# Two dense expert loops: the order of their VectorE and ScalarE work around the gate multiply

## The chip, the cores and the metric

The kernel runs on one core of a Trainium2 chip. The metric is the device time of a launch in microseconds: 2806.3 us, the median of three runs (2805.26 to 2808.78). The engines are named TensorE (PE; PEld is its weight load), VectorE (DVE), ScalarE (ACT), GpSimd (POOL) and SyncE (SP). Each engine works through its own instructions in order and waits at the head of its queue.

## The reference, cut to what matters

Two layers, each a token mixer and then PEER, a feed-forward part with 16384 experts. A token picks 128 experts (8 heads, 16 each):

```python
eidx = jnp.take_along_axis(cidx, pos, axis=-1)
gate = jax.nn.softmax(best, axis=-1)
ue = jnp.take(u, eidx, axis=0)
ve = jnp.take(v, eidx, axis=0)
act = jax.nn.gelu(jnp.einsum('td,thkd->thk', xc, ue).astype(jnp.float32)) * gate
return jnp.einsum('thk,thkd->td', act.astype(xc.dtype), ve)
```

u and v are 16384 x 1024 in float32. Layer 0 has 512 tokens (256 of the context, 256 latent), layer 1 only the 256 latent ones.

## The kernel before

The kernel does most tokens **densely**: the gates are spread into a matrix over all experts that is zero where an expert wasn't picked, and then all 16384 experts are computed for all tokens, 128 experts at a time. `dense` does this in 128 steps n. In layer 0 three tiles of 128 tokens go this way (nd = 3, 384 columns) and the fourth is gathered; in layer 1 both tiles are dense (nd = 2, 256 columns).

The matmuls take float32 in pieces: a value x becomes a high part, which ScalarE writes as a rounded copy, and a low part, which VectorE writes as x less the high part. `mm3` (L109 to L111) adds three products: high by high, high by low, low by high. One step n has these parts:

- `part(n)`: uh (ScalarE, L719) and ul (VectorE, L720) from 128 x 1024 values of u; two buffers each.
- `dots(n)`: 24 matmuls of u with the tokens' high and low parts into the tile mm.
- `act(n)`: ScalarE writes c = gelu(mm) (L735).
- `gated(n)`: VectorE multiplies c by the gates (L903); then ch (ScalarE, L65) and cl (VectorE, L73); two buffers each.
- `partv(n)`: vh (ScalarE, L880) and vl (VectorE, L881) from v. vh has three buffers; vl has two in layer 0 and three in layer 1.
- `second(n)`: 18 matmuls in layer 0 and 12 in layer 1, of ch and cl with vh and vl, added up in PSUM over all 128 steps. The first load of each three takes ch, the second matmul vl, the third load cl.

The order within a loop is written out by hand (`manual_schedule`). Step n issues dots(n+3) and act(n+3), gated(n+1), part(n+5), second(n) and partv(n+2).

**Stashed columns.** For some n, c was computed before the loop, in gaps of earlier stages, and kept in DRAM: 20 in layer 0 (n = 10, 11, 22, 23, 36, 37, 48, 49, 62, 63, 74, 75, 86, 87, 100, 101, 112, 113, 126, 127) and 32 in layer 1 (6, 7, 14, 15 and so on to 126, 127). They come in pairs; for them the loop leaves part and dots out and SyncE loads c (L873).

**Gather steps.** In layer 0 the fourth tile's experts are gathered, one row pair of u and v a token, in 131 gather steps put between the dense steps. A gather step e takes a piece of the top-k work for the next head (`pick`), adds v of an earlier expert (`accum`, VectorE, L827), starts a gather (`fetch`, GpSimd, L811) and takes the dot product of the tokens with a gathered row of u (`dot`, VectorE, L817), whose sum two small ScalarE instructions turn into a coefficient (L818, L819). After each dense step a formula says how many of them are issued: one after most, none after some, two after the steps 6, 31, 46, 70, 95 and 110. The last item is `combine` for this tile, with its transposes on TensorE, after step 124.

SyncE loads u and v two steps at a time, 1024 KB each (L711, L862), into a ring of five buffers that both share, and the gates (L868).

Of the kernel before, what the change touches and what calls it, by code (L numbers as in the profile page):

```python
# [37 lines left out]
class Kern:  # L38
# [664 lines left out]
    def first_half(self, l, ND, hh, hl, b):  # L703
# [10 lines left out]

        def part(n, eng=None):

            t, x = U.pop(n)
            uh, ul = b([128, 8, 128], F32R, tag="uh", bufs=2), b([128, 8, 128], F32R, tag="ul", bufs=2)
            nc.scalar.activation(uh, t[:, x], AF.Copy)  # L719
            (eng or nc.vector).tensor_tensor(ul, t[:, x], uh.bitcast(F32), op=ALU.subtract)  # L720
            return uh, ul

# [14 lines left out]

        return load, part, dots, act, hold

    def dense(self, l, t0, nd, hh, hl, IX, GA, first, stash, waits, spare, ng, gather):  # L740
# [3 lines left out]
        with ExitStack() as st:  # L744
# [43 lines left out]

            gsteps = []
            if gather:  # L790
# [23 lines left out]
                def dot(e):  # L814
                    x = UV[e]
                    a = gp([128, 1], F32, tag="act", bufs=3)
                    nc.vector.scalar_tensor_tensor(x[:, 0:1024], x[:, 0:1024], 1.0, htok, op0=ALU.mult, op1=ALU.mult, accum_out=a)  # L817
                    nc.scalar.activation(a, a, AF.Gelu_apprx_tanh)  # L818
                    nc.scalar.activation(a, a, AF.Copy, scale=gGA[:, e:e + 1])  # L819
                    ACT[e] = a  # L820

                def accum(e):
                    x, a = UV.pop(e)[:, 1024:2048], ACT.pop(e)
                    if e == 0:
# [51 lines left out]

            def partv(n):
                vh, vl = b2([128, 1024], F32R, tag="vh", bufs=3), b2([128, 1024], F32R, tag="vl", bufs=2 if nd == 3 else 3)
                v = V.pop(n)
                nc.scalar.activation(vh, v, AF.Copy)  # L880
                nc.vector.tensor_tensor(vl, v, vh.bitcast(F32), op=ALU.subtract)  # L881
                return vh, vl

# [6 lines left out]
            with self.tc.manual_schedule():  # L890
# [8 lines left out]

                def gated(n):  # L900
                    c = C.pop(n)
                    cv = c.rearrange("p (c t) -> p c t", t=32)
                    nc.vector.tensor_mul(cv, cv, GT.pop(n))  # L903
                    ch, cl = b2([128, ND], F32R, tag="ch", bufs=2), b2([128, ND], F32R, tag="cl", bufs=2)
                    self.split(c, ch, cl)
                    S[n] = (ch, cl)

                for n in range(3):
                    C[n] = act(dots(P.pop(n)))
                    P[n + 2] = part(n + 2)  # L910
                    if n < 2:
                        VV[n] = partv(n)
                for n in range(128):
                    loadg(n + 4)
                    loadv(n + 4)
                    if n + 6 not in late:
                        load(n + 6)
                    if n == 0:
                        gated(0)
                    if n + 3 < 128 and n + 3 not in late:  # L920
                        C[n + 3] = act(dots(P.pop(n + 3)))
                    if n + 1 < 128:
                        gated(n + 1)
                    if n + 5 < 128 and n + 5 not in late:
                        P[n + 5] = part(n + 5)
                    second(n, S.pop(n), VV.pop(n))
                    if n + 2 < 128:
                        VV[n + 2] = partv(n + 2)
                    spent += 0.9 if n in late else 2
                    while gsteps and ns - len(gsteps) < (ns + 2) * spent / total:  # L930
                        gsteps.pop(0)()
            for x in gsteps:
                x()
# [298 lines left out]
```

## Time and profile before

| | |
|---|---|
| median of 3 runs | 2806.3 us |
| the profiled execution | 2807.95 us, of which its span is 2806.2 us |
| TensorE busy | 2673.5 us (95%) |
| its weight loads | 2305.6 us (82%) |
| VectorE | 2028.2 us (72%) |
| ScalarE | 1412.6 us (50%) |
| GpSimd | 572.8 us (20%) |
| granted TensorE clock | 0.985 of full speed |

Busy shares are means over stages with different limits: the two dense loops are the stretches from 718 to 1708 us and from 2181 to 2796 us, and each has to be read for itself. A matmul's end is modelled and overlaps the next one's start, so how TensorE paces is best read from the starts of its weight loads. In brackets behind a row stands the time in which the engine was idle before that instruction, and what ended it.

### The profile page before, as it was taken

To read this page: it belongs to the slowest core of one execution; us is meant where nothing else is said; L and a number is where in the kernel's file an instruction comes from. 1 tells how busy PE (TensorE), PEld (TensorE's weight loads), DVE (VectorE), ACT (ScalarE), POOL (GpSimd) and SP (SyncE) were. 2 spreads that over 40 slices of the span, in tenths; PEclk is the share of its full clock that TensorE was granted. 3 is DMA by queue.
4 is the path that set the end of the run, shared out by engine and by line. 5 is a ranking of instruction groups with operands and counts; after the bars stand their busy time and mean duration, and the time that the engine had idled before them with its cause. 6 is when DMAs were issued, how large, how long until landed. Compare 5 with 4: busy or idle time off the path is not lost.

```text
span 2806.2 us, 40422 instructions
## 1 busy us (share of the span) xinstructions
PE 2673.5 (95%) x15043; PEld 2305.6 (82%) x15043; DVE 2028.2 (72%) x4323; ACT 1412.6 (50%) x2528; POOL 572.8 (20%) x538
## 2 busy tenths in 40 slices
PE   7999999999999999999999998998889999999998
PEld 4677778798988888898898896657789888888887
DVE  4688559999677787787878776656987655555555
ACT  5756543399444344444344436444388444444444
POOL 0000023288122222221222221005366000000000
PEclk9999999999999999999999999999999999999999
DMA  6334223445788878887778782354346665666653
GB/s 257 126 135 149 91 79 147 150 195 225 271 296 300 302 272 300 299 303 280 283 289 313 298 298 77 120 216 148 124 184 253 240 220 212 226 233 220 218 216 126
DMA packets 155204, 609.68 MB, mean 217 GB/s; under 512 B 10752, under 2 KB 90368, under 8 KB 90880
## 3 DMA queue, kind: packets, MB, share of 16 engines
q1 hardware_dynamic: 136576, 472.87, 46.0%
q0 software_dynamic: 18432, 134.23, 13.1%
q8 instruction: 119, 1.95, 0.3%
q14 instruction: 77, 0.63, 0.1%
HBM read 555.94 MB, written 51.12 MB: 216 GB/s over the span
## 4 chain that ended last, share of the span: by engine, by line
PE 47%; issue 22%; DVE 13%; POOL 12%; ACT 3%; DMA 1%; POOLq 0%; DVEq 0%; ACTq 0%
POOL uv L811 6%; POOL o L778 6%; PE t L109 6%; PE t L111 6%; PE t L110 6%; PE mm L111 5%; PE mm L109 5%; PE mm L110 5%; PE pj L111 2%; PE pj L109 2%; PE pj L110 2%; PE gp L780 2%; PE mm L168 1%; DVE eq L568 1%; PE pj L1065 1%
## 5 line engine op out<-in xcount | busy, mean ns | idle before, releaser
L109 PE MATMUL mm<-t,uh 128*128 128x384 f32 (+1 forms) x2048 | 637.1, 311 | 5.6 <-ACT c L735 3.0
L111 PE MATMUL mm<-t,ul 128*128 128x384 f32 (+1 forms) x2048 | 636.6, 311 | 2.2 <-POOL ul L720 2.2
L110 PE MATMUL mm<-t,uh 128*128 128x384 f32 (+1 forms) x2048 | 635.4, 310 | 0.1
L109 PE MATMUL t<-vh,ch 128*128 128x512 f32 x1280 | 502.4, 392 | 21.1 <-ACT ch L65 21.1
L111 PE MATMUL t<-vh,cl 128*128 128x512 f32 x1280 | 503.7, 394 | 0.0
L110 PE MATMUL t<-vl,ch 128*128 128x512 f32 x1280 | 501.6, 392 | 0.0
L109 PEld LDWEIGHTS mm<-t,uh 128*128 128x128 f32 x2048 | 387.0, 189 | 15.2 <-ACT c L735 3.7
L110 PEld LDWEIGHTS mm<-t,uh 128*128 128x128 f32 x2048 | 387.2, 189 | 9.2 <-DVE t L214 0.3
L111 PEld LDWEIGHTS mm<-t,ul 128*128 128x128 f32 x2048 | 387.2, 189 | 3.1 <-POOL ul L720 3.0
L720 DVE TENSOR_TENSOR ul<-r,uh 128x1024 fp32r<-128x1024 f32 x229 | 280.4, 1225 | 132.6 <-ACT uh L719 132.2
L811 POOL DMA_INDIRECT uv<-in_uv_dram,t x128 | 211.4, 1651 | 763.2 <-DVE t L827 715.8
L881 DVE TENSOR_TENSOR vl<-r,vh 128x1024 fp32r<-128x1024 f32 x256 | 312.6, 1221 | 73.3 <-PE t L110 51.0
L73 DVE TENSOR_TENSOR cl<-c,ch 128x384 fp32r<-128x384 f32 (+1 forms) x256 | 125.9, 492 | 308.0 <-ACT ch L65 308.0
L818 ACT ACTIVATE act<-act 128x1 f32<-128x1 f32 x128 | 26.0, 203 | 546.5 <-DVE uv L817 546.5
L109 PEld LDWEIGHTS t<-vh,ch 128*128 128x128 f32 x1280 | 241.4, 189 | 70.9 <-ACT ch L65 27.4
L719 ACT ACTIVATE uh<-r 128x1024 fp32r<-128x1024 f32 x256 | 270.4, 1056 | 52.3 <-PE mm L110 26.1
L111 PEld LDWEIGHTS t<-vh,cl 128*128 128x128 f32 x1280 | 241.0, 188 | 56.0 <-DVE cl L73 5.0
L110 PEld LDWEIGHTS t<-vl,ch 128*128 128x128 f32 x1280 | 240.9, 188 | 44.1
L880 ACT ACTIVATE vh<-r 128x1024 fp32r<-128x1024 f32 x256 | 268.8, 1050 | 0.0
L735 ACT ACTIVATE c<-mm 128x384 f32<-128x384 f32 (+1 forms) x256 | 110.7, 433 | 281.7 <-PE mm L111 280.4
L778 POOL TENSOR_SCALAR o<-t,trs 128x128 f32<-128x128 f32 x320 | 215.8, 693 | 52.8 <-ACT trs L757 45.8
L779 DVE TENSOR_SCALAR o<-t,trs 128x128 f32<-128x128 f32 x640 | 184.8, 362 | 0.0
(323 smaller groups left out, 4513.2 us busy)
## 6 DMA issues: line engine op xcount, KB each, us to landing
r<-in_ut_dram SPq DMA_DIRECT2D x128, 1024.0 KB
r<-in_vv_dram SPq DMA_DIRECT2D x128, 1024.0 KB
r<-in_wm_dram SPq DMA_DIRECT2D x48, 1024.0 KB
t<-buf SPq DMA_DIRECT2D x20, 2048.0 KB
gates<-t SPq DMA_DIRECT2D x32, 768.0 KB
r<-in_wq_dram SPq DMA_DIRECT2D x16, 1024.0 KB
gates<-t SPq DMA_DIRECT2D x16, 1024.0 KB
r<-in_ew_dram SPq DMA_DIRECT2D x14, 1024.0 KB
```

The lines of the kernel that those rows point to most:

```text
L73: e[1].tensor_tensor(lo, x, hi.bitcast(F32), op=ALU.subtract)
L109: mm(p, a[0], b[0], start=first, stop=False)
L110: mm(p, a[0], b[1], start=False, stop=False)
L111: mm(p, a[1], b[0], start=False, stop=last)
L719: nc.scalar.activation(uh, t[:, x], AF.Copy)
L720: (eng or nc.vector).tensor_tensor(ul, t[:, x], uh.bitcast(F32), op=ALU.subtract)
L735: nc.scalar.activation(a, p, AF.Gelu_apprx_tanh)
L778: nc.gpsimd.tensor_scalar(o1, self.iota, trs[:, 0, tk:tk + 1], None, op0=ALU.is_equal)
L779: nc.vector.tensor_scalar(o2, self.iota, trs[:, 1, tk:tk + 1], trs[:, 2, tk:tk + 1], op0=ALU.is_equal, op1=ALU.mult)
L811: nc.gpsimd.indirect_dma_start(out=UV[e], out_offset=None, in_=i[f"uv{l}"], in_offset=bass.IndirectOffsetOnAxis(ap=EI[:, e:e + 1], axis=0))
L880: nc.scalar.activation(vh, v, AF.Copy)
L881: nc.vector.tensor_tensor(vl, v, vh.bitcast(F32), op=ALU.subtract)
```

## The change

`part`, `partv` and `gated` are each cut in two: `part_hi` and `part_lo`, `partv_hi` and `partv_lo`, and `gate`, `gated_hi` and `gated_lo`. Step n now issues, in this order: dots(n+3); the gate multiply of n+1; ul of n+4; ch of n+1; what the gather steps left for ScalarE; vh of n+2; uh of n+5; the gelu of n+3; cl of n+1; vl of n+1; second(n). So uh runs one step ahead of ul, and vh one step ahead of vl. The two small ScalarE instructions behind a gather's dot product are put on a list (`defer`) and issued at `flush`, or at the next `accum` if that comes first. Gate, ch and cl of n = 0 come ahead of the loop.

```diff
-        def part(n, eng=None):
+        def part_hi(n):
             t, x = U.pop(n)
             uh, ul = b([128, 8, 128], F32R, tag="uh", bufs=2), b([128, 8, 128], F32R, tag="ul", bufs=2)
             nc.scalar.activation(uh, t[:, x], AF.Copy)
-            (eng or nc.vector).tensor_tensor(ul, t[:, x], uh.bitcast(F32), op=ALU.subtract)
-            return uh, ul
+            return uh, ul, t[:, x]
+
+        def part_lo(u, eng=None):
+            (eng or nc.vector).tensor_tensor(u[1], u[2], u[0].bitcast(F32), op=ALU.subtract)
+            return u[:2]
...
-                    nc.scalar.activation(a, a, AF.Gelu_apprx_tanh)
-                    nc.scalar.activation(a, a, AF.Copy, scale=gGA[:, e:e + 1])
                     ACT[e] = a
+                    def rest():
+                        nc.scalar.activation(a, a, AF.Gelu_apprx_tanh)
+                        nc.scalar.activation(a, a, AF.Copy, scale=gGA[:, e:e + 1])
+                    defer.append(rest)
...
                 for n in range(128):
                     loadg(n + 4)
                     loadv(n + 4)
                     if n + 6 not in late:
                         load(n + 6)
-                    if n == 0:
-                        gated(0)
-                    if n + 3 < 128 and n + 3 not in late:
-                        C[n + 3] = act(dots(P.pop(n + 3)))
+                    a = n + 3 < 128 and n + 3 not in late
+                    p = dots(P.pop(n + 3)) if a else None
                     if n + 1 < 128:
-                        gated(n + 1)
+                        gate(n + 1)
+                    if n + 4 in P:
+                        P[n + 4] = part_lo(P[n + 4])
+                    x = gated_hi(n + 1) if n + 1 < 128 else None
+                    flush()
+                    if n + 2 < 128:
+                        VV[n + 2] = partv_hi(n + 2)
                     if n + 5 < 128 and n + 5 not in late:
-                        P[n + 5] = part(n + 5)
+                        P[n + 5] = part_hi(n + 5)
+                    if a:
+                        C[n + 3] = act(p)
+                    if x:
+                        gated_lo(*x)
+                        VV[n + 1] = partv_lo(VV[n + 1])
                     second(n, S.pop(n), VV.pop(n))
-                    if n + 2 < 128:
-                        VV[n + 2] = partv(n + 2)
```

The rows of TensorE, SyncE and GpSimd stand in the same order before and after. VectorE in an ordinary step of layer 0, from the gate multiply of n = 13 to that of n = 14; before:

```order
L903 TENSOR_TENSOR c_7709<-c_7709,gates_7567 128x384
L73 TENSOR_TENSOR cl_7848<-c_7709,ch_7847 128x384
L720 TENSOR_TENSOR ul_7852<-r_7682,uh_7851 128x1024
L881 TENSOR_TENSOR vl_7874<-r_7680,vh_7873 128x1024
L827 SCALAR_TENSOR_TENSOR t_2576<-uv_7607,act_7809,t_2576 128x1024
L817 SCALAR_TENSOR_TENSOR uv_7674,act_7880<-uv_7674,t_2572 128x1024
L903 TENSOR_TENSOR c_7767<-c_7767,gates_7567 128x384
```

and of the change (c_7718 and c_7776 are the same two columns):

```order
L921 TENSOR_TENSOR c_7718<-c_7718,gates_7563 128x384
L724 TENSOR_TENSOR ul_7774<-r_7678,uh_7773 128x1024
L929 TENSOR_TENSOR cl_7843<-c_7718,ch_7842 128x384
L899 TENSOR_TENSOR vl_7771<-r_7565,vh_7770 128x1024
L840 SCALAR_TENSOR_TENSOR t_2576<-uv_7605,act_7807,t_2576 128x1024
L824 SCALAR_TENSOR_TENSOR uv_7672,act_7878<-uv_7672,t_2572 128x1024
L921 TENSOR_TENSOR c_7776<-c_7776,gates_7563 128x384
```

ul moved from behind cl to between the gate multiply and cl, and is that of n = 16 (before, 17); vl is that of n = 13 (before, 14).

ScalarE in the same step, before:

```order
L735 ACTIVATE c_7844<-mm_7819 128x384
L65 ACTIVATE ch_7847<-c_7709 128x384
L719 ACTIVATE uh_7851<-r_7682 128x1024
L880 ACTIVATE vh_7873<-r_7680 128x1024
L818 ACTIVATE act_7880<-act_7880 128x1
L819 ACTIVATE act_7880<-act_7880,t_2574 128x1
```

and of the change:

```order
L925 ACTIVATE ch_7842<-c_7718 128x384
L828 ACT_TABLE_LOAD
L828 ACTIVATE act_7807<-act_7807 128x1
L829 ACTIVATE act_7807<-act_7807,t_2574 128x1
L895 ACTIVATE vh_7847<-r_7676 128x1024
L719 ACTIVATE uh_7850<-r_7678 128x1024
L742 ACTIVATE c_7853<-mm_7815 128x384
```

The gelu moved from the front of the step to its end, and the two small instructions behind a dot product to behind the next step's ch (the table load stands before too, one row above).

VectorE at the first pair of stashed columns, from vl of n = 8 to cl of n = 8, with two gather steps in between; before:

```order
L881 TENSOR_TENSOR vl_7496<-r_7303,vh_7495 128x1024
L548 MATCH_REPLACE cand_7364<-best_7428,cand_7364 128x136
L549 MAX best_7428<-cand_7364 128x8
L550 MAX_INDEX pos_7429<-best_7428,cand_7364 128x8
L827 SCALAR_TENSOR_TENSOR t_2576<-uv_7295,act_7435,t_2576 128x1024
L817 SCALAR_TENSOR_TENSOR uv_7368,act_7505<-uv_7368,t_2572 128x1024
L552 TENSOR_TENSOR t_2574<-best_7428 128x16
L827 SCALAR_TENSOR_TENSOR t_2576<-uv_7368,act_7505,t_2576 128x1024
L817 SCALAR_TENSOR_TENSOR uv_7433,act_7513<-uv_7433,t_2572 128x1024
L903 TENSOR_TENSOR c_7399<-c_7399,gates_7301 128x384
L73 TENSOR_TENSOR cl_7521<-c_7399,ch_7520 128x384
```

and of the change, where vl_7403 is that of n = 7 and vl_7474 that of n = 8:

```order
L899 TENSOR_TENSOR vl_7403<-r_7157,vh_7402 128x1024
L548 MATCH_REPLACE cand_7362<-best_7427,cand_7362 128x136
L549 MAX best_7427<-cand_7362 128x8
L550 MAX_INDEX pos_7428<-best_7427,cand_7362 128x8
L840 SCALAR_TENSOR_TENSOR t_2576<-uv_7293,act_7434,t_2576 128x1024
L824 SCALAR_TENSOR_TENSOR uv_7366,act_7504<-uv_7366,t_2572 128x1024
L552 TENSOR_TENSOR t_2574<-best_7427 128x16
L840 SCALAR_TENSOR_TENSOR t_2576<-uv_7366,act_7504,t_2576 128x1024
L824 SCALAR_TENSOR_TENSOR uv_7432,act_7512<-uv_7432,t_2572 128x1024
L921 TENSOR_TENSOR c_7405<-c_7405,gates_7297 128x384
L929 TENSOR_TENSOR cl_7518<-c_7405,ch_7517 128x384
L899 TENSOR_TENSOR vl_7474<-r_7299,vh_7473 128x1024
```

vl of n = 8 moved from ahead of these gather steps, the gate multiply and cl to behind all of them; vl of n = 7 stands in its old place.

## Rows read from the trace of the kernel before

**Rows 1.** Both loops: us; busy PE, PEld, DVE, ACT, POOL (instructions); clock; DMA share, GB/s.
```profile
718.20:1694.00 975.80, 955.91 (x4751) 856.76 (x4751) 757.28 (x1154) 399.51 (x739) 211.35 (x128) 1.00 0.79 292
2181.30:2795.80 614.50, 613.87 (x3747) 549.30 (x3746) 356.05 (x475) 287.89 (x440) 0.00 (x0) 1.00 0.60 214
```

**Rows 2.** Waits of the weight loads, 718 to 1700: total us, times, longest.
```profile
PEld t L109 <- ACT ch L65: 26.6, 16, 4.9
PEld t L111 <- DVE cl L73: 4.5, 15, 0.5
```

**Rows 3.** Waits of the weight loads, 2160 to 2796 us.
```profile
PEld t L109 <- ACT ch L65: 0.8, 1, 0.8
```

**Rows 4.** Timeline of weight loads, one ordinary step; start, us, instruction.
```profile
904.61 0.19 PEld L109 LDWEIGHTS mm<-t,uh 128*128 128x128 f32 x1
...
908.85 0.19 PEld L109 LDWEIGHTS t<-vh,ch 128*128 128x128 f32 x1
...
912.89 0.19 PEld L109 LDWEIGHTS mm<-t,uh 128*128 128x128 f32 x1
```

**Rows 5.** Timeline of weight loads, layer 0: loop start, combine (8 loads), last stall, end.
```profile
714.04 0.19 PEld L109 LDWEIGHTS mm<-t,uh 128*128 128x128 f32 x1
...
1693.53 1.02 PEld L690 LDWEIGHTS mm<-t,t 128*128 128x128 f32 x8
...
1699.47 0.19 PEld L109 LDWEIGHTS t<-vh,ch 128*128 128x128 f32 x1 [0.99 <-ACT ch L65]
...
1707.69 0.14 PEld L690 LDWEIGHTS mm<-t,gates 128*128 128x128 f32 x1
```

**Rows 6.** Timeline of weight loads at the first pair: second(6), second(8), dots(12).
```profile
768.31 0.19 PEld L109 LDWEIGHTS t<-vh,ch 128*128 128x128 f32 x1
...
781.33 0.19 PEld L109 LDWEIGHTS t<-vh,ch 128*128 128x128 f32 x1 [4.95 <-ACT ch L65]
...
787.00 0.19 PEld L109 LDWEIGHTS mm<-t,uh 128*128 128x128 f32 x1
```

**Rows 7.** Stretch after that stall, columns as in rows 1.
```profile
781.40:785.30 3.90, 3.90 (x10) 2.93 (x11) 3.44 (x10) 1.78 (x2) 0.00 (x0) 0.56 1.03 429
```

**Rows 8.** Timeline of VectorE at the first pair, vl(8) to gate(9).
```profile
772.60 1.22 DVE L881 TENSOR_TENSOR vl<-r,vh 128x1024 fp32r<-128x1024 f32 x1 [2.14 <-PE t L110]
...
780.11 0.56 DVE L903 TENSOR_TENSOR c<-c,gates 128x384 f32<-128x384 f32 x1
781.32 0.56 DVE L73 TENSOR_TENSOR cl<-c,ch 128x384 fp32r<-128x384 f32 x1 [0.65 <-ACT ch L65]
...
783.41 1.22 DVE L881 TENSOR_TENSOR vl<-r,vh 128x1024 fp32r<-128x1024 f32 x1
...
787.63 0.56 DVE L903 TENSOR_TENSOR c<-c,gates 128x384 f32<-128x384 f32 x1
```

**Rows 9.** Timeline of VectorE over the two gather steps after step 46.
```profile
1086.85 1.22 DVE L881 TENSOR_TENSOR vl<-r,vh 128x1024 fp32r<-128x1024 f32 x1
...
1094.25 0.55 DVE L903 TENSOR_TENSOR c<-c,gates 128x384 f32<-128x384 f32 x1
```

**Rows 10.** Gathers: the last line of the view of tile uv.
```profile
DMA to landing us min/median/max: 5.5/6.6/11.9
```

**Rows 11.** Timeline of GpSimd: two gathers' issue.
```profile
725.41 0.94 POOL L811 DMA_INDIRECT uv<-in_uv_dram,t  x1 [0.30 <-issue]
...
776.29 1.68 POOL L811 DMA_INDIRECT uv<-in_uv_dram,t  x1 [6.98 <-DVE t L827]
```

**Rows 12.** Timeline in layer 1 at a pair: three second, then dots.
```profile
2193.47 0.19 PEld L109 LDWEIGHTS t<-vh,ch 128*128 128x128 f32 x1
...
2197.20 0.42 ACT L65 ACTIVATE ch<-c 128x256 fp32r<-128x256 f32 x1 [1.71 <-DVE c L903]
...
2197.65 0.43 DVE L73 TENSOR_TENSOR cl<-c,ch 128x256 fp32r<-128x256 f32 x1 [0.56 <-ACT ch L65]
...
2201.57 0.19 PEld L109 LDWEIGHTS mm<-t,uh 128*128 128x128 f32 x1
```

More of the change, by code (lines that the diff above doesn't have):

```diff
@@ L719, in part @@
             nc.scalar.activation(uh, t[:, x], AF.Copy)
-            (eng or nc.vector).tensor_tensor(ul, t[:, x], uh.bitcast(F32), op=ALU.subtract)
-            return uh, ul
+            return uh, ul, t[:, x]
+        def part_lo(u, eng=None):
+            (eng or nc.vector).tensor_tensor(u[1], u[2], u[0].bitcast(F32), op=ALU.subtract)
+            return u[:2]
+        def part(n, eng=None):
+            return part_lo(part_hi(n), eng)
         def dots(u):
@@ L736, in act @@
             return a
-        return load, part, dots, act, hold
+        return load, part, dots, act, hold, part_hi, part_lo
     def dense(self, l, t0, nd, hh, hl, IX, GA, first, stash, waits, spare, ng, gather):
@@ L817, in dot @@
                     nc.vector.scalar_tensor_tensor(x[:, 0:1024], x[:, 0:1024], 1.0, htok, op0=ALU.mult, op1=ALU.mult, accum_out=a)
-                    nc.scalar.activation(a, a, AF.Gelu_apprx_tanh)
-                    nc.scalar.activation(a, a, AF.Copy, scale=gGA[:, e:e + 1])
                     ACT[e] = a
+                    def rest():
+                        nc.scalar.activation(a, a, AF.Gelu_apprx_tanh)
+                        nc.scalar.activation(a, a, AF.Copy, scale=gGA[:, e:e + 1])
+                    defer.append(rest)
                 def accum(e):
+                    while defer:
+                        defer.pop(0)()
                     x, a = UV.pop(e)[:, 1024:2048], ACT.pop(e)
@@ L875, in dense, with partv_hi @@
             late = set(waits)
-            def partv(n):
+            part_hi, part_lo = first[5:]
+            def partv_hi(n):
                 vh, vl = b2([128, 1024], F32R, tag="vh", bufs=3), b2([128, 1024], F32R, tag="vl", bufs=2 if nd == 3 else 3)
@@ L880, in partv, with partv_lo @@
                 nc.scalar.activation(vh, v, AF.Copy)
-                nc.vector.tensor_tensor(vl, v, vh.bitcast(F32), op=ALU.subtract)
-                return vh, vl
+                return vh, vl, v
+            def partv_lo(x):
+                nc.vector.tensor_tensor(x[1], x[2], x[0].bitcast(F32), op=ALU.subtract)
+                return x[:2]
             def second(n, c, v):
@@ L898, in dense, with gate, gated_hi, gated_lo @@
                 loadg(0)
-                def gated(n):
-                    c = C.pop(n)
+                def gate(n):
+                    c = C[n]
                     cv = c.rearrange("p (c t) -> p c t", t=32)
                     nc.vector.tensor_mul(cv, cv, GT.pop(n))
-                    ch, cl = b2([128, ND], F32R, tag="ch", bufs=2), b2([128, ND], F32R, tag="cl", bufs=2)
-                    self.split(c, ch, cl)
-                    S[n] = (ch, cl)
+                def gated_hi(n):
+                    S[n] = x = b2([128, ND], F32R, tag="ch", bufs=2), b2([128, ND], F32R, tag="cl", bufs=2)
+                    nc.scalar.activation(x[0], C[n], AF.Copy)
+                    return C.pop(n), x
+                def gated_lo(c, x):
+                    nc.vector.tensor_tensor(x[1], c, x[0].bitcast(F32), op=ALU.subtract)
+                def flush():
+                    while defer:
+                        defer.pop(0)()
                 for n in range(3):
                     C[n] = act(dots(P.pop(n)))
-                    P[n + 2] = part(n + 2)
+                    P[n + 2] = part_hi(n + 2)
                     if n < 2:
-                        VV[n] = partv(n)
+                        P[n + 2] = part_lo(P[n + 2])
+                        VV[n] = partv_hi(n)
+                VV[0] = partv_lo(VV[0])
+                gate(0)
+                gated_lo(*gated_hi(0))
                 for n in range(128):
```

3 lines of the change are left out of this document (2 added, 1 removed).

## The prediction

> **What bounds the kernel now.** I read the view by stretches first. Each dense loop is a stretch of its own: layer 0 runs from 718 to 1694 us, layer 1 from 2181 to 2796 [rows 1]. The reader is to see how little there is to win. TensorE is busy 613.9 of 614.5 us in layer 1 and 955.9 of 975.8 us in layer 0, while VectorE and ScalarE have room in both. So only the time in which TensorE waits in layer 0's loop can be saved, and everything else that the change moves is cover. The second view is that of the waits of the weight loads, which start each matmul: in layer 0 they waited 26.6 us in 16 places for ch (ScalarE) and 4.5 us in 15 places for cl (VectorE) [rows 2]; in layer 1 once, 0.8 us, at the loop's start [rows 3].
>
> The third view, the timeline of the weight loads, gives the full price. In an ordinary step dots(n+3) takes 908.85 - 904.61 = 4.24 us and second(n) 912.89 - 908.85 = 4.04 us [rows 4]. Layer 0's loop goes from 714.04 to 1707.69 us, with 1.02 us for combine's transposes at 1693.53 [rows 5]: 992.6 us without them. It holds 105 dots (128 less 20 stashed, less 3 ahead of it) and 128 second; 23 of these have no dots in front, and I count them at 4.09. 105 x 4.24 + 105 x 4.04 + 23 x 4.09 = 963.5 us. So **29.1 us are lost** in layer 0; this holds the clock too, which fell to 1.2 GHz for a moment after the longest stall (0.56 granted over 3.9 us, [rows 7]).
>
> Where they are lost: at the pairs of stashed columns, every 12 steps or so. Call such a pair a and a+1. dots(a) and dots(a+1) are left out, so second(a-4), (a-3) and (a-2) run back to back: TensorE takes two steps in 8.1 us that take 16.6 elsewhere. In the first pair (a = 10) second(6) starts at 768.31, and second(8) is due at 768.31 + 4.04 + 4.09 = 776.44. It starts at 781.33, after waiting 4.95 us for ch(8), and the next dots starts at 787.00 instead of 780.53 [rows 6]: 6.5 us lost. VectorE's rows say why [rows 8]. vl(8) stands at the head of its queue and waits 2.14 us for second(6) to let go of its buffer (vl has two here). Behind it, in the order of the code, stand two gather steps and then gate(8), which begins at 780.11, and cl(8) at 781.32. Work that has 8 us to spare stands in front of work that has none.
>
> **The change, part by part.** No operation is added or removed; TensorE, SyncE and GpSimd issue the same rows in the same order. Only VectorE and ScalarE are reordered, inside the two loops. So matmuls, transfers and gathers cost what they cost; what changes is who stands in front of whom.
>
> *vl behind cl.* vl(n+2) was issued in step n and waited there for second(n); vl(n+1) is now issued in step n behind cl(n+1), which waits for the same second(n-1) through ch (two buffers). The wait stays, but gate(n+1) stands ahead of it. For the first pair, with rows' durations: second(5) ends at 768.31 - 4.24 = 764.07, and a waiter starts 0.25 us later (second(6) ends at 772.35, vl at 772.60). ch(7) is then at 764.3, cl(7) 0.6 later at 764.9, vl(7) at 765.4. From vl to the next gate over two gather steps there are 780.11 - 772.60 = 7.51 us [rows 8], so gate(8) starts at 772.9 instead of 780.1. cl(8) follows 1.21 later (781.32 - 780.11) at 774.1, vl(8) at 774.6, done at 775.8. Due is 776.44: no stall, 0.6 us to spare. The other pairs have one gather step at that place, or have the double one earlier, and more room: the stalls of this kind go.
>
> *ul a step later.* ul(n+4) is now computed in step n and needed by dots(n+4) in step n+1, one step less ahead. In an ordinary step that is still 8 us. At a pair: vl(8) at 774.6, then one gather step with its pieces of top-k, 787.63 - 783.41 = 4.22, so gate(9) at 778.8 and ul(12) from 779.3 to 780.5. dots(12) is due at 780.53 and needs ul at its third load, 0.35 later: covered by 0.4 us. Where two gather steps fall on a-2 (a = 48 and 112) the queue is longer. With second(a-4)'s end as 0: vl(a-2) at 1.3, gate(a-1) at 1.3 + 3.6 to 4.2 = 4.9 to 5.5, ul(a+2) behind it, vl(a-1) at 7.0 to 7.7, the double step 1094.25 - 1086.85 = 7.40 [rows 9], gate(a) at 14.4 to 15.1, ul(a+3) done at 16.1 to 16.8. Due is 4.09 + 4.09 + 4.24 + 4.04 + 0.35 = 16.8. Nothing to spare; with a gather landing late (5.5 to 11.9 us, median 6.6, [rows 10], against some 10 us that the code leaves in such a pair) up to 2 us are lost in each of the two. I take 1 us per place there, 2 in all; bounds 0 and 5.
>
> *uh, vh, gelu and the held-back activation.* ScalarE issues ch first, then the gather's two small activations, vh, uh and last the gelu. It is busy 399.5 of 975.8 us; gelu of n+3 is needed by gate(n+3) two steps on. Cost 0. If that cover were gone, ch would be late behind uh: 1 us at each of 10 pairs, 10 in all.
>
> *u and v held longer.* The subtraction reads the raw u and v later, so a ring slot frees later. The load that waits in SyncE's queue behind it is u(m+6), which waits for vl(m+1): before, 1.3 us after second(m-1) at the earliest, now 2.3. uh(m+6) comes 8.28 + 4.24 = 12.5 us after second(m-1), so a lead of 11.2 becomes 10.2. Cost 0; bound 5.
>
> *Start and end.* ch(0) and cl(0) are ready ahead of second(0): layer 1 wins its 0.8 [rows 3], within the bounds 0 and 1.2. At the end of layer 0 combine's work stands ahead of gate(126) and TensorE waits 0.99 us [rows 5]; that stays, with vl(126) now behind it too: 1 us kept of the 29.1, bounds 0 and 2.
>
> *Layer 1.* TensorE is full there, so it can only lose. A tight place is again second(a-2), here with (2201.57 - 2193.47) / 3 = 2.70 us per second [rows 12]. Behind second(a-4): 0.25 to ch, 0.45 to cl (2197.65 - 2197.20), 0.35 to vl, 1.22 for it: 2.3 us, and vl is needed at the second matmul, about 3.1. It fits by 0.8. Cost 0; if not, each us over costs 1 us at 16 pairs and at 5 seconds at the end.
>
> **Sum**: 29.1 + 0.8 - 2 - 1 = 27 us. The profiled execution took 2807.95 us (span 2806.2), which gives 2781; it stands 1.65 above the median of the three runs, so the forecast for a median is **2779.5 us**.
>
> **A page against it.** GpSimd's issue of a gather takes 0.94 us beside a vl subtraction and 1.68 beside the dot product [rows 11]. The Trainium skill, "SBUF — State Buffer", section "SBUF: two separate sides", says that VectorE and GpSimd share a port pair under an exclusive lock, taken also by VectorE operations with two SBUF inputs, and that the descriptors of a gather are starved by it; a VectorE with fewer gaps would then hold the gathers up. By that rule each gather would start one 1.22 us operation later and the two crowded pairs would lose 1.2 us more each, 2782. The rows beside vl don't show such a hold, and dot still follows accum, so I leave the sum as it is.
>
> **Rivals.**
> 1. *The subtraction ends last at the pairs.* The stall on ch is replaced by one on vl or ul. For it: only 0.4 to 0.6 us are to spare in the first pair. Against it: most pairs have single steps. At 1 us at 8 more pairs and 2 more at the two crowded ones, 12 us are given back: 2791.
> 2. *VectorE is the bound there anyway,* and the stalls only change their name. For it: VectorE works 757 of 976 us, with little slack where steps are short. Against it: it waits between gate and cl, and 2.14 us for vl in the very stretch. The gain stays under 5 us: 2803.
> 3. *Layer 1 pays (slower).* Chain ch, cl, vl behind second(a-4) is longer than 3.1 us, so that TensorE, full today, stalls at 16 pairs and 5 places at the end. It decides from 0.8 us more than I count; at 1.5 us over it costs 21 x 1.5 = 32, and with half of layer 0's gain given back (13 kept) the time is 2825. Against it: each link has its row, and vl has three buffers there.
>
> **How the numbers follow.** Forecast 0.75, with its own range 2775 to 2785 (all of it won, or 5 us more given back); rival 1 0.13; rival 2 0.06; rival 3 0.06. Below 2774 nothing is left to win. The range that leaves out 2 in 10 reaches into rival 1: 2774 to 2793. About 0.2% (5.6 us) can be told from no change: faster is the forecast and rival 1 and a little of rival 2, 0.89; same most of rival 2, 0.05; slower 0.06.
>
> **What would show it.** Waits of the weight loads for ch and cl in layer 0 fall from 31 us to under 5; the steps at pairs keep their 4.09; no clock drop inside the loop. VectorE's wait for "PE t" moves from vl to ch on ScalarE. Wrong would be: weight loads or matmuls that wait for vl or ul at the pairs (rival 1); a gate that still starts after second is due (rival 2); TensorE below 99.5% in layer 1 (rival 3).

## Result and the profile after

The changed kernel takes **2780.3 us** (median of four runs, 2778.8 to 2782.2), the kernel before 2807.5 (2805.3 to 2810.2): a ratio of 0.9906 (0.9892 to 0.9919), 27.2 us saved. The forecast was 2779.5. The profiled execution took 2781.66 us, with a span of 2779.9.

The view by stretches, for the same two stretches as [rows 1]: us; busy PE, PEld, DVE, ACT, POOL (instructions); clock; DMA share, GB/s.

```profile
720.14:1668.20 948.06, 946.81 (x4751) 856.75 (x4751) 742.18 (x1153) 404.53 (x738) 211.42 (x128) 1.00 0.83 300
2154.80:2769.30 614.50, 614.50 (x3754) 550.28 (x3753) 350.42 (x475) 296.34 (x440) 0.00 (x0) 1.00 0.61 214
```

TensorE now has 1.25 us left in which it isn't busy in layer 0, where it had 19.9, and none in layer 1. The engines do the same work as before; the stretch is 27.7 us shorter. What is left shows in the waits of the weight loads, layer 0's stretch first (answers to [rows 2]): total us, times, longest.

```profile
PEld mm L111 <- DVE ul L724: 1.6, 1, 1.6
PEld t L110 <- DVE vl L899: 0.9, 1, 0.9
```

The 31.1 us for ch and cl are gone. In layer 1 the 0.8 us of [rows 3] are gone too. The timeline of weight loads gives the loop's length (answers to [rows 5]): the start of dots(3), combine's transposes, the last stall, the end.

```profile
715.98 0.19 PEld L109 LDWEIGHTS mm<-t,uh 128*128 128x128 f32 x1
...
1667.71 1.02 PEld L690 LDWEIGHTS mm<-t,t 128*128 128x128 f32 x8
...
1673.83 0.19 PEld L110 LDWEIGHTS t<-vl,ch 128*128 128x128 f32 x1 [0.94 <-DVE vl L899]
...
1681.67 1.02 PEld L690 LDWEIGHTS mm<-t,gates 128*128 128x128 f32 x8
```

965.69 us, 27.96 less than the 993.65 of before. So the account of the two profiled executions is: 1.94 us later into the loop (dots(3) at 715.98 instead of 714.04; over all the runs here second(0) begins between 717.8 and 720.9), 27.96 gained in it, 0.8 at layer 1's start, and 0.5 lost outside the loops: 0.3 between them (from layer 0's end to layer 1's first load of ch it is 474.10 us, before 474.59, where 0.8 less was due) and 0.3 behind layer 1's last load of ch. That makes 26.3 us in all.

At the first pair of stashed columns, weight loads of second(6), (7), (8) and dots(12), against [rows 6]:

```profile
769.78 0.19 PEld L109 LDWEIGHTS t<-vh,ch 128*128 128x128 f32 x1
...
773.82 0.19 PEld L109 LDWEIGHTS t<-vh,ch 128*128 128x128 f32 x1
...
777.90 0.19 PEld L109 LDWEIGHTS t<-vh,ch 128*128 128x128 f32 x1
...
781.98 0.19 PEld L109 LDWEIGHTS mm<-t,uh 128*128 128x128 f32 x1
```

Three second in 12.20 us without a gap; before, 18.69. VectorE there, against [rows 8]: vl(7), gate(8), cl(8), vl(8), gate(9), ul(12).

```profile
766.77 1.22 DVE L899 TENSOR_TENSOR vl<-r,vh 128x1024 fp32r<-128x1024 f32 x1
...
774.28 0.56 DVE L921 TENSOR_TENSOR c<-c,gates 128x384 f32<-128x384 f32 x1
775.49 0.56 DVE L929 TENSOR_TENSOR cl<-c,ch 128x384 fp32r<-128x384 f32 x1 [0.65 <-ACT ch L925]
775.96 1.22 DVE L899 TENSOR_TENSOR vl<-r,vh 128x1024 fp32r<-128x1024 f32 x1
...
780.60 0.56 DVE L921 TENSOR_TENSOR c<-c,gates 128x384 f32<-128x384 f32 x1
781.07 1.22 DVE L724 TENSOR_TENSOR ul<-r,uh 128x1024 fp32r<-128x1024 f32 x1
```

gate(8) begins 4.5 us after second(6) where it began 11.8 after it, and cl(8) begins 2.4 us ahead of second(8). And ScalarE's queue at the same place: ch(7), the gelu of n = 9, ch(8).

```profile
765.74 0.52 ACT L925 ACTIVATE ch<-c 128x384 fp32r<-128x384 f32 x1 [3.37 <-PE t L110]
...
770.15 0.49 ACT L742 ACTIVATE c<-mm 128x384 f32<-128x384 f32 x1 [2.51 <-PE mm L111]
...
774.93 0.53 ACT L925 ACTIVATE ch<-c 128x384 fp32r<-128x384 f32 x1 [3.03 <-DVE c L921]
```

The reader is to see the first two: ch(7) goes as soon as second(5) has let go of its buffer, and only then does ScalarE wait for dots(9) to write the gelu. The experiments show that about half of the gain hangs on this place of the gelu.

VectorE's two longest waits in layer 0 after the change (total, times, longest):

```profile
DVE cl L929 <- ACT ch L925: 138.6, 69, 3.8
DVE sm L578 <- ACT t L576: 30.7, 7, 5.0
```

The second is new and is in no row of before. It is the softmax of the gathered tile's gates: once a head VectorE waits for the Exp, which now stands behind ch, vh and uh in ScalarE's queue. At one pair (a = 74; a and a+1 are the stashed columns of a pair) this reaches TensorE. ScalarE (the table load, with the Exp right behind it), VectorE and then the weight load there:

```profile
1265.31 1.28 ACT L576 ACT_TABLE_LOAD   x1
```

```profile
1266.86 0.17 DVE L578 TENSOR_REDUCE sm<-t 128x1 f32<-128x16 f32 x1 [2.15 <-ACT t L576]
...
1270.25 1.22 DVE L724 TENSOR_TENSOR ul<-r,uh 128x1024 fp32r<-128x1024 f32 x1
```

```profile
1271.52 0.19 PEld L111 LDWEIGHTS mm<-t,ul 128*128 128x128 f32 x1 [1.56 <-DVE ul L724]
```

ul is late by the 2.15 us that VectorE lost, less 0.6 that it had to spare.

### The profile page after: what moved, and what is told of

It is laid out like the page before. It is cut to its first block, busy times and chain, and to the rows that moved or that the text cites. A ratio compares the mean times of both kernels' runs of the same rounds, so it can differ in the third digit from the quotient of the medians.

```text
span 2779.9 us, 40556 instructions
## 1 busy us (share of the span) xinstructions
PE 2665.7 (96%) x15043; PEld 2307.9 (83%) x15043; DVE 2003.6 (72%) x4323; ACT 1426.6 (51%) x2528; POOL 573.1 (21%) x538
## 3 DMA queue, kind: packets, MB, share of 16 engines
q0 software_dynamic: 18432, 134.23, 13.3%
## 4 chain that ended last, share of the span: by engine, by line
PE 74%; DVE 14%; POOL 5%; ACT 4%; issue 1%; DMA 0%; POOLq 0%; ACTq 0%; DVEq 0%
PE t L110 10%; PE t L111 10%; PE t L109 10%; PE mm L111 9%; PE mm L109 9%; PE mm L110 9%; POOL o L785 4%; PE gp L787 2%; PE pj L111 2%; PE pj L109 2%; PE pj L110 2%; PE mm L168 1%; DVE eq L568 1%; PE mm L1143 1%; PE pj L1106 1%
## 5 line engine op out<-in xcount | busy, mean ns | idle before, releaser
L925 ACT ACTIVATE ch<-c 128x384 fp32r<-128x384 f32 (+1 forms) x256 | 120.8, 472 | 518.2 <-PE t L110 263.8
L818 POOL DMA_INDIRECT uv<-in_uv_dram,t x128 | 211.4, 1652 | 728.5 <-DVE t L840 685.5
L724 POOL TENSOR_TENSOR ul<-r,uh 128x1024 fp32r<-128x1024 f32 x27 | 66.3, 2458 | 581.9 <-PE mm L189 367.6
```

Of the source, the lines that this page charges most:

```text
L724: (eng or nc.vector).tensor_tensor(u[1], u[2], u[0].bitcast(F32), op=ALU.subtract)
L818: nc.gpsimd.indirect_dma_start(out=UV[e], out_offset=None, in_=i[f"uv{l}"], in_offset=bass.IndirectOffsetOnAxis(ap=EI[:, e:e + 1], axis=0))
L925: nc.scalar.activation(x[0], C[n], AF.Copy)
```

## Experiments

All runs in one table: the median, the ratio to the kernel before on the same chip with its interval, and each loop's length in the profiled execution, from the first to the last weight load of ch. The kernel before had medians of 2807.5 us beside the change and 2806.7, 2806.2 and 2808.5 us in the three groups, and loops of 988.6 and 613.0 us.

| run | median us | ratio (interval) | layer 0 | layer 1 |
|---|---|---|---|---|
| the change | 2780.3 | 0.9906 (0.9892 to 0.9919) | 960.9 | 613.0 |
| vl_only | 2846.9 | 1.0147 (1.0129 to 1.0166) | 1002.7 | 637.3 |
| all_but_vl | 2846.2 | 1.0144 (1.0126 to 1.0162) | 1027.4 | 613.0 |
| gather_first | 2898.9 | 1.0328 (1.0310 to 1.0346) | 1078.9 | 613.0 |
| gate_early | 2826.4 | 1.0069 (1.0051 to 1.0087) | 1006.2 | 613.2 |
| u_whole | 2781.0 | 0.9911 (0.9895 to 0.9928) | 959.4 | 613.0 |
| no_defer | 2778.1 | 0.9900 (0.9884 to 0.9917) | 960.5 | 613.0 |
| exp_gate | 2775.6 | 0.9889 (0.9872 to 0.9905) | 959.1 | 613.0 |
| after_again | 2779.3 | 0.9906 (0.9889 to 0.9922) | 960.9 | 613.0 |
| gelu_front | 2794.7 | 0.9947 (0.9931 to 0.9964) | 977.0 | 613.0 |
| gelu_only | 2811.1 | 1.0007 (0.9997 to 1.0017) | 992.2 | 613.0 |
| vl_ul | 2804.9 | 0.9987 (0.9978 to 0.9997) | 980.9 | 618.4 |
| vl_gelu | 2787.0 | 0.9922 (0.9906 to 0.9939) | 964.3 | 617.2 |

Some of these kernels lose time where a loop starts, and some at the pairs. So here the loops once more, cut at second(5) in layer 0 and at second(3) in layer 1, in us between first loads of ch:

| run | layer 0: second(0) to (5) | (5) to (127) | layer 1: second(0) to (3) | (3) to (127) |
|---|---|---|---|---|
| before | 41.6 | 943.6 | 13.9 | 597.1 |
| the change | 41.4 | 916.1 | 13.9 | 597.1 |
| vl_only | 48.3 | 951.1 | 19.6 | 615.7 |
| gelu_front | 41.4 | 932.2 | 13.9 | 597.1 |
| gelu_only | 41.6 | 947.2 | 13.8 | 597.1 |
| vl_ul | 46.6 | 930.9 | 19.3 | 597.1 |
| vl_gelu | 46.3 | 914.6 | 18.1 | 597.1 |

### First group: is vl's place in VectorE's queue the whole cause?

The prediction's cause was that vl, at the head of VectorE's queue, holds up the gather steps and the gate. Four kernels were to show that by itself. All four were slower than before, and outside the times expected.

**vl_only**: the kernel before, with vl(n+1) behind cl(n+1) and nothing else moved (so the gelu stays in front, and ul between cl and vl).

```diff
+            def partv_lo(x):
+                nc.vector.tensor_tensor(x[1], x[2], x[0].bitcast(F32), op=ALU.subtract)
+                return x[:2]
...
                     if n + 5 < 128 and n + 5 not in late:
                         P[n + 5] = part(n + 5)
+                    if n == 0:
+                        VV[0] = partv_lo(VV[0])
+                    if n + 1 < 128:
+                        VV[n + 1] = partv_lo(VV[n + 1])
                     second(n, S.pop(n), VV.pop(n))
```

> The kernel before with one move: vl of n+1 behind cl of n+1, as in the change; all else in the old order. Theory A (vl of n+2, which waits for second(n), stood in front of the gather steps, the gate multiply and cl): nearly the whole gain, 2781 to 2786 us, with small waits for vl at the pairs with a double gather step, since ul stands between cl and vl here. Rival B (the gain is from ul placed between the gate multiply and cl, so that VectorE does not stand idle for ch): 2800 us or more.

It is 40 us slower than before: 14 in layer 0, 24 in layer 1. Of these, 12.4 us go at the two loops' starts, for a reason that has nothing to do with the pairs: this edit writes vl(0) in step 0, behind gate(1), cl(1) and ul(5), where before it was ready ahead of the loop, and second(0) waits for it (5.37 us in layer 0, 4.46 in layer 1). Behind the starts layer 0 is 7.5 us longer than before and layer 1 18.6. In layer 0 at the first pair, ScalarE:

```profile
777.27 0.49 ACT L735 ACTIVATE c<-mm 128x384 f32<-128x384 f32 x1 [2.13 <-PE mm L111]
777.65 0.52 ACT L65 ACTIVATE ch<-c 128x384 fp32r<-128x384 f32 x1
```

second(5) was over at 772.66, where the loads of dots(9) begin, so ch(7) could have gone at 772.9. But the gelu stands ahead of it and waits for dots(9): ch(7) is 4.7 us late, and with it cl, vl, both gather steps and the gate. VectorE and the weight loads then:

```profile
786.18 0.56 DVE L906 TENSOR_TENSOR c<-c,gates 128x384 f32<-128x384 f32 x1
787.39 0.56 DVE L73 TENSOR_TENSOR cl<-c,ch 128x384 fp32r<-128x384 f32 x1 [0.65 <-ACT ch L65]
788.34 1.22 DVE L720 TENSOR_TENSOR ul<-r,uh 128x1024 fp32r<-128x1024 f32 x1 [0.39 <-ACT uh L719]
789.48 1.22 DVE L884 TENSOR_TENSOR vl<-r,vh 128x1024 fp32r<-128x1024 f32 x1
```

```profile
787.41 0.27 PEld L109 LDWEIGHTS t<-vh,ch 128*128 128x128 f32 x1 [2.43 <-ACT ch L65]
790.75 0.29 PEld L110 LDWEIGHTS t<-vl,ch 128*128 128x128 f32 x1 [3.08 <-DVE vl L884]
```

Two stalls where the kernel before had one of 4.95: a shorter one for ch, and one for vl behind ul, which itself waited for uh. In layer 1 only the second kind shows, 1.36 us at each of 15 pairs; VectorE at one of them, and the load that waits:

```profile
2257.18 0.43 DVE L73 TENSOR_TENSOR cl<-c,ch 128x256 fp32r<-128x256 f32 x1 [0.56 <-ACT ch L65]
2258.13 1.23 DVE L720 TENSOR_TENSOR ul<-r,uh 128x1024 fp32r<-128x1024 f32 x1 [0.53 <-ACT uh L719]
2259.27 1.22 DVE L884 TENSOR_TENSOR vl<-r,vh 128x1024 fp32r<-128x1024 f32 x1
```

```profile
2260.54 0.19 PEld L110 LDWEIGHTS t<-vl,ch 128*128 128x128 f32 x1 [1.36 <-DVE vl L884]
```

vl starts 2.09 us after cl instead of 0.35. That is rival 3's mechanism, with one more link in the chain.

**all_but_vl**: the change, but vh and vl of n+2 whole behind second(n), as before.

```diff
-                VV[0] = partv_lo(VV[0])
...
-                    if n + 2 < 128:
-                        VV[n + 2] = partv_hi(n + 2)
...
                     if x:
                         gated_lo(*x)
-                        VV[n + 1] = partv_lo(VV[n + 1])
                     second(n, S.pop(n), VV.pop(n))
+                    if n + 2 < 128:
+                        VV[n + 2] = partv_hi(n + 2)
```

(`partv_hi` there writes vh and vl, as `partv` did.)

> The change with vh and vl of n+2 put back together behind second(n), ul still between gate and cl, activations still held back. Theory A: the stalls at the pairs are back, weight loads wait some 25 to 40 us for ch, cl or ul in layer 0, 2803 to 2815 us. Rival B: most of the gain stays, under 2790 us.

Slower by 40 us, all in layer 0, and some 30 us beyond the range: the stalls that theory A expected are back, but for ul they are larger. The waits of its weight loads:

```profile
PEld mm L111 <- DVE ul L724: 32.2, 22, 3.2
PEld t L109 <- ACT ch L922: 27.0, 13, 4.9
```

The 27 us for ch are as large as in [rows 2]: without the vl move they stay. The other 32 are the price of ul(n+4) standing behind the late gate, one step nearer to the dots that needs it.

**gather_first**: the kernel before, with the gather steps ahead of vh and vl.

```diff
-                    if n + 2 < 128:
-                        VV[n + 2] = partv(n + 2)
                     spent += 0.9 if n in late else 2
                     while gsteps and ns - len(gsteps) < (ns + 2) * spent / total:
                         gsteps.pop(0)()
+                    if n + 2 < 128:
+                        VV[n + 2] = partv(n + 2)
```

> The kernel before with the gather steps issued ahead of vh and vl of n+2 in place of behind them; nothing else. Theory A: vl's wait for second(n) then has only gate and cl behind it, which come 0.25 + 1.1 + 1.2 us after second(n), so the stalls at the pairs go: 2780 to 2787 us. Rival B: no change, 2804 to 2810 us.

The slowest of all, by 92 us, and not at pairs alone: the weight loads wait 94.2 us for ch, at 56 places. ScalarE and VectorE in an ordinary step:

```profile
909.15 0.20 ACT L818 ACTIVATE act<-act 128x1 f32<-128x1 f32 x1 [4.64 <-DVE uv L817]
909.38 0.29 ACT L819 ACTIVATE act<-act,t 128x1 f32<-128x1 f32 x1
909.59 1.04 ACT L880 ACTIVATE vh<-r 128x1024 fp32r<-128x1024 f32 x1
```

```profile
910.66 1.23 DVE L881 TENSOR_TENSOR vl<-r,vh 128x1024 fp32r<-128x1024 f32 x1 [1.54 <-ACT vh L880]
```

vh now stands on ScalarE behind the two small instructions that wait for the dot product, and VectorE waits for it at 116 places, 178.1 us in all.

**gate_early**: the kernel before, with gate(n+2) right behind vl(n+2), ahead of the gather steps.

```diff
                 def gated(n):
                     c = C.pop(n)
-                    cv = c.rearrange("p (c t) -> p c t", t=32)
-                    nc.vector.tensor_mul(cv, cv, GT.pop(n))
...
                     if n + 2 < 128:
                         VV[n + 2] = partv(n + 2)
+                        gate(n + 2)
```

(The two lines taken out of `gated` are what `gate` does; gates 0 and 1 are done in step 0.)

> The kernel before with the gate multiply of n+2 issued right behind vl of n+2, ahead of the gather steps; cl stays behind them. Theory A: ch is early but cl still waits behind the gather steps; each stall shrinks by 1.1 us (the 1.21 from gate to cl less the lead of the third load), so the two long ones stay at 3.8 us, in all some 12 of 26 us are left: 2790 to 2796 us, and the weight loads wait for cl, not ch. A rival C (the gate multiply alone is late): all stalls gone, 2778 to 2783 us.

Slower by 20 us. At the first pair the gate is early, at 776.19, but ScalarE reads:

```profile
783.60 0.20 ACT L818 ACTIVATE act<-act 128x1 f32<-128x1 f32 x1 [2.95 <-DVE uv L817]
783.84 0.29 ACT L819 ACTIVATE act<-act,t 128x1 f32<-128x1 f32 x1
784.04 0.51 ACT L65 ACTIVATE ch<-c 128x384 fp32r<-128x384 f32 x1
```

ch still comes behind the gather's small instructions, so behind the dot product. ch(8) begins 13.3 us after second(6) (770.76), where it began 12.4 after it in the kernel before, and the weight loads wait 35.8 us for ch at 16 places instead of 26.6. An earlier gate wins nothing as long as ch stands where it stands.

So theory A, that VectorE's order alone decides, fell. In three of the four ScalarE's order stood in the way: ch behind a gelu that waits for dots (vl_only), vh and ch behind the small instructions that wait for a dot product (gather_first, gate_early). all_but_vl agrees with one half of it: without vl's move the stalls for ch stay.

### Second group: what the change doesn't need

**u_whole**: the change, with ul(n+5) behind vl(n+1) in the step that writes uh(n+5), so that u isn't a step apart.

```diff
-                    if n + 4 in P:
-                        P[n + 4] = part_lo(P[n + 4])
...
                         VV[n + 1] = partv_lo(VV[n + 1])
+                    if n + 5 < 128 and n + 5 not in late:
+                        P[n + 5] = part_lo(P[n + 5])
```

> The change with uh and ul of n+5 in the same step again, ul behind vl of n+1. Theory A: ul's place does not matter, it has a step to spare: 2777 to 2784 us. Rival B (ul between gate and cl is what wins): 2790 us or more.

**no_defer**: the change, with the gather's two small instructions issued at once.

```diff
-                    defer.append(rest)
+                    rest()
```

> The change without holding back: the two small ScalarE instructions behind a dot product are issued at once, at the end of the step. Theory A: they only stand ahead of the next step's ch, which waits for second anyway: 2777 to 2784 us. Rival D (ScalarE's order matters, ch is held up by a dot product of the gather): some of the stalls come back, 2788 us or more.

**after_again**: the change itself, beside them.

> The change itself again beside the others, as their reference: 2780 us.

2781.0, 2778.1 and 2779.3 us, with loops within 1.5 us of each other: neither ul's new place between gate and cl nor the held-back activations carry more of the gain than the 3 us by which these three differ.

**exp_gate**: the change, with the Exp one gather step ahead of the rest of the softmax, and gate(126) ahead of combine.

```diff
-                    softmax(gGA[:, None, hs], 1, gp)
+                    g = gGA[:, None, hs]
+                    nc.scalar.activation(g, g, AF.Exp)
+                    yield
+                    softmax(g, 1, gp, False)
...
-                    if n + 1 < 128:
+                    if n + 1 < 128 and n != 125:
                         gate(n + 1)
...
                     second(n, S.pop(n), VV.pop(n))
+                    if n == 124:
+                        gate(126)
```

> The change with two more moves: the exponential of a head's softmax one gather step ahead of the rest of it, and gate of n = 126 ahead of combine after step 124. The change still had two stalls in layer 0, 1.6 us for ul behind a softmax that waits for ScalarE, and 0.9 us for vl behind combine. Expected: both gone, 2.5 us faster than the change, about 2778 us. If the stall for ul has another cause (a gather that lands late), only 0.9 us.

Both of the change's remaining stalls are smaller: none for ul, and 0.6 us for vl at the end.

2775.6 us (2774.3 to 2777.3): each of its four times is below each of after_again's (2778.4 to 2782.5), though their intervals against the kernel before overlap. The loop is 1.7 us shorter. It is the fastest version run.

### Third group: vl and the gelu together

Theory E: the gain takes two moves, vl behind cl on VectorE and the gelu behind ch on ScalarE, and either alone gives next to nothing. Three kernels add them to the kernel before, one takes the gelu out of the change.

**gelu_front**: the change, with the gelu of n+3 right behind dots(n+3).

```diff
-                    p = dots(P.pop(n + 3)) if a else None
+                    if a:
+                        C[n + 3] = act(dots(P.pop(n + 3)))
...
-                    if a:
-                        C[n + 3] = act(p)
                     if x:
                         gated_lo(*x)
```

> The change with the gelu of n+3 back in its old place, right behind dots(n+3) and so ahead of ch of n+1 on ScalarE; all else as in the change. Theory E (vl behind cl helps only if ch need not stand behind a gelu that waits for dots of the same step): cl and vl start 4.24 us later in every step with dots, the pairs with a double gather step stall again for 2 to 4 us, 2788 to 2800 us, layer 1 unharmed. The prediction's reckoning (the gelu's place costs and wins nothing): 2777 to 2784 us.

About half is given back: it saves 13.8 us beside the kernel before where the change saves 27, and its loop is 16 us longer. The range of E held; its words that either move alone gives next to nothing did not: vl's move keeps half of the gain with the gelu in its old place. ScalarE at the first pair:

```profile
767.81 0.49 ACT L742 ACTIVATE c<-mm 128x384 f32<-128x384 f32 x1 [6.00 <-PE mm L111]
768.20 0.51 ACT L925 ACTIVATE ch<-c 128x384 fp32r<-128x384 f32 x1
```

second(6) begins at 767.44, so ch(7) comes behind its start, where the change has it 4.04 us ahead of it (765.74 against 769.78). TensorE then waits 2.42 us for ch(8) and 1.54 for vl(8).

**gelu_only**: the kernel before, with the gelu behind ch and uh.

```diff
-                    if n + 3 < 128 and n + 3 not in late:
-                        C[n + 3] = act(dots(P.pop(n + 3)))
+                    a = n + 3 < 128 and n + 3 not in late
+                    p = dots(P.pop(n + 3)) if a else None
...
                         P[n + 5] = part(n + 5)
+                    if a:
+                        C[n + 3] = act(p)
```

> The kernel before with one move: the gelu of n+3 behind ch of n+1 and uh of n+5. Theory E: vl of n+2 still waits for second(n) ahead of the gather steps and the gate multiply, so the stalls at the pairs stay: 2800 to 2809 us. Rival F (the gelu's place alone is the whole gain): 2777 to 2785 us.

Nothing gained, 2 us above the expected range; its waits for ch are those of before (26.3 us at 15 places): ch(8) waits for gate(8), and that still stands behind vl(8).

**vl_ul**: the kernel before, with vl(n+1) behind cl and ul(n+5) behind vl; the gelu in front. (`part` and `partv` are cut in two as in the change.)

```diff
...
-                        P[n + 5] = part(n + 5)
+                        P[n + 5] = part_hi(n + 5)
+                    if n == 0:
+                        VV[0] = partv_lo(VV[0])
+                    if n + 1 < 128:
+                        VV[n + 1] = partv_lo(VV[n + 1])
+                    if n + 5 in P:
+                        P[n + 5] = part_lo(P[n + 5])
```

> As vl_gelu, but with the gelu in front as before: vl of n+1 behind cl, ul of n+5 behind vl. Against vl_only it shows what ul between cl and vl cost: layer 1 is back at 613 us, since the chain behind second is ch, cl, vl again (2.3 us in place of 3.9, against 3.1 to spare). Layer 0 still stalls at the pairs, since ch waits behind the gelu: 2798 to 2812 us. Rival (vl_only's loss in layer 1 has another cause): 2825 us or more.

Against vl_only, layer 1 falls from 637.3 to 618.4 us: ul between cl and vl cost it 19 us. It isn't back at 613, as expected, since its start still loses 5.5 us; behind the start it is. Layer 0 keeps the gelu's stalls. The median alone would make vl's move look worth 3.6 us. But 10.5 us go at the two starts, where second(0) waits for vl(0) as in vl_only; behind the start layer 0 takes 930.9 us instead of 943.6, so **vl's move alone is worth 12.7 us at the pairs**, as in gelu_front (11.4).

**vl_gelu**: vl_ul and gelu_only together.

```diff
-                    if n + 3 < 128 and n + 3 not in late:
-                        C[n + 3] = act(dots(P.pop(n + 3)))
+                    a = n + 3 < 128 and n + 3 not in late
+                    p = dots(P.pop(n + 3)) if a else None
...
-                        P[n + 5] = part(n + 5)
+                        P[n + 5] = part_hi(n + 5)
+                    if a:
+                        C[n + 3] = act(p)
+                    if n == 0:
+                        VV[0] = partv_lo(VV[0])
+                    if n + 1 < 128:
+                        VV[n + 1] = partv_lo(VV[n + 1])
+                    if n + 5 in P:
+                        P[n + 5] = part_lo(P[n + 5])
```

> The kernel before with the two moves together: vl of n+1 behind cl (ul of n+5 behind vl), and the gelu of n+3 behind ch and uh. No ul a step apart, no work between gate and cl, nothing held back. Theory E: these two are the gain, 2777 to 2786 us. If more parts are needed, over 2795 us.

1 us above the expected range in the median. Beside the kernel before (2808.5), gelu_only is 2.6 us slower, vl_ul 3.6 faster, and both together 21.5 faster. Behind the start of layer 0, where the loss at the starts doesn't blur it, gelu_only is 3.6 us longer than before, vl_ul 12.7 shorter and vl_gelu 29.0 shorter: the gelu's move costs a little by itself and is worth 16.3 us once vl has moved. There vl_gelu (914.6 us) has all that the change has (916.1, with its stall at a = 74). What is missing to the change stands at the two loops' starts, where vl(0) is written in step 0 and not ahead of it; they take 9.2 us more than in the change. That is more than the waits alone: after the first of them the granted clock was 0.60 from 722 to 726 us. No run has vl_gelu with vl(0) ahead of the loop.

```profile
721.74 0.19 PEld L110 LDWEIGHTS t<-vl,ch 128*128 128x128 f32 x1 [3.39 <-DVE vl L893]
...
2158.34 0.19 PEld L110 LDWEIGHTS t<-vl,ch 128*128 128x128 f32 x1 [2.71 <-DVE vl L893]
```

At the pairs it has no stall.

## Why the prediction was right, and where it wasn't

- *What bounds the kernel, and how much there is*: right. 29.1 us were counted as lost in layer 0; 27.96 came back, and the waits that remain are 2.5 us. So the count of the least time (963.5 us) was about 1.3 us too high. The sum has a slip: 2781 less 1.65 is 2779.35, not 2779.5. That the forecast came within 0.8 us is in part luck: the loop won 1.9 us more than the 26.1 counted for it, and in the profiled execution it began 1.94 us later.
- *vl behind cl*: right in time and place. With second(6) at 769.78 instead of 768.31, 1.47 later, the prediction reads gate(8) 774.4, cl(8) 775.6, vl(8) 776.1, gate(9) 780.3, ul(12) 780.8; measured are 774.28, 775.49, 775.96, 780.60 and 781.07. VectorE's wait for `PE t` moved from vl to ch on ScalarE, as foretold: 51.0 us at 46 places were vl's before, none are after, and ScalarE's ch waits 185.4 us at 71.
- *uh, vh, gelu and the held-back activation: "Cost 0"*: **this step failed as a reason.** It asked only whether the gelu would still be early enough for its own reader. What counts is who stands behind it: in its old place it waits for dots(n+3) with ch(n+1) behind it. While vl stood ahead of the gate that cost nothing (gelu_only); once vl stands behind cl, it is 13 to 16 us (gelu_front; 16.3 from vl_ul to vl_gelu). The working for vl quietly used the new place, in taking ch(7) at 0.25 us after second(5). The forecast of the whole change came out because both moves are in it; a forecast for vl alone, made with the same reason, was wrong by over 60 us (vl_only), though not for this alone: 12.4 us went at the starts and 18.6 for ul ahead of vl in layer 1.
- *Two crowded pairs, 2 us*: 0. At a = 48, with second(44)'s end as 0 (1063.0 us, from dots(50) at 1071.20 less two second), the prediction had vl(47) at 7.0 to 7.7 and gate(48) at 14.4 to 15.1; the rows have 6.8 and 14.2, and no gather was waited for there:

```profile
1069.82 1.22 DVE L899 TENSOR_TENSOR vl<-r,vh 128x1024 fp32r<-128x1024 f32 x1
...
1077.21 0.55 DVE L921 TENSOR_TENSOR c<-c,gates 128x384 f32<-128x384 f32 x1
```

- Instead 1.6 us went at a = 74, for a cause that the prediction didn't have: the Exp behind vh and uh. "Cost 0" for ScalarE again left out who waits behind; exp_gate removes it.
- *The end*: 0.94 us, now for vl, where 1 was counted. *The start*: layer 1 won its 0.8. *Layer 1* (rival 3): no stall; it does pay when the chain behind second(a-4) gets one link longer (vl_only, 18.6 us behind the start). Its rows make the margin smaller than the 0.8 us counted: 1.74 more between cl and vl cost 1.36 at a pair, so some 0.4 were to spare.
- *u and v held longer*: neither ScalarE nor a weight load waits for a transfer of u or v inside the loop. Nothing lost.
- *Rivals 1 and 2*: vl and ul end last at two places, 2.5 us, not 12; VectorE is not the bound, its 742 us of work fit into 948.
- *The page against it*: the gathers cost nothing more, but not for the reason given. [rows 11] were misread: at 725.41 VectorE is not at vl, it is at an operation with one input:

```profile
725.35 0.29 DVE L518 MAX8 sv<-t 128x8 f32<-128x128 f32 x1
```

The rows do show the hold. In the kernel before, all 123 issues that began during a dot product, which has two inputs in SBUF, took 1.67 to 1.75 us and ended 0.8 us after it; the three that began while VectorE had no such operation, or just as one ended (725.41 is one), took 0.94; two that began late in a subtraction took 1.06 and 1.16. After the change one issue began 0.22 us into a subtraction, and it took longest of all, until 1.03 us after that one's end:

```profile
726.57 1.22 DVE L724 TENSOR_TENSOR ul<-r,uh 128x1024 fp32r<-128x1024 f32 x1
```

```profile
726.79 2.03 POOL L818 DMA_INDIRECT uv<-in_uv_dram,t  x1 [25.14 <-DVE c L921]
```

The Trainium skill, "SBUF — State Buffer", section "SBUF: two separate sides", has VectorE operations with two SBUF inputs hold the ports that they share with GpSimd only against a GpSimd operation that reads SBUF; the trace agrees, if a gather's issue counts as one (its column of indices lies there). What the section says of starved descriptors, it says of VectorE's two-port modes, not of these subtractions. The change lost nothing by it, since the hold is as long as before: in both kernels a gather is issued when accum is done, and the dot product comes next. After the change the issue has a mean of 1652 ns, before 1651, and the gathers land as fast as in [rows 10]:

```profile
L818 POOL DMA_INDIRECT uv<-in_uv_dram,t x128 | 211.4, 1652 | 728.5 <-DVE t L840 685.5
```

```profile
DMA to landing us min/median/max: 5.6/6.5/12.1
```

VectorE did wait for a gather at three places, 6.8 us in all, where it was 0.5 at one before; no weight load waited behind them.

What stays open: how the 13 to 16 us of gelu_front divide into waiting and into the clock, which fell there in two spells (0.83 granted from 775 to 785 us, 0.98 from 1200 to 1300).

## What to carry to other kernels

Before an instruction is moved on one in-order engine, write down for each engine what stands behind it, and check that its inputs come from a queue whose order allows the new place. A wait that costs nothing while something later ends last becomes the bound when that is removed: price moves together, and time each alone and both. Read such runs by stretches: what vl_ul won at the pairs was hidden in its total by what its edit lost at the loops' starts. An instruction with much slack itself (a gelu needed two steps on) may be the one that has to move, for the sake of the one behind it.

## What the runs showed that was not expected

Moving one subtraction on VectorE, with no work added, made the kernel 40 us slower, and putting the gather steps ahead of it 92 us slower: the two engines' orders are coupled so closely that half a reordering can be worse than none. After the change VectorE waits 30.7 us over seven heads for an Exp that stands late in ScalarE's queue, and one such wait reaches TensorE. The table load ahead of that Exp takes 1.28 us (1265.31); the Trainium skill, "ScalarE: Activation LUTs", section "What ACT_TABLE_LOAD costs", has 1283 ns, which agrees.
